# A second pair of buffers for the weights of a filler, and two more for the probabilities

## The chip, the cores and the metric

The kernel runs on one core of a Trainium2 chip, as one program. The metric is the time of one execution on the device in microseconds (us). Its engines are TensorE (PE, with its weight loads as PEld), VectorE (DVE), ScalarE (ACT) and GpSimd (POOL); SyncE (SP) issues the transfers. Each has its own queue of instructions and runs it in order, and semaphores make one wait for another.

## What is computed

One step of a small diffusion backbone with two layers, over 256 context tokens and 1024 latent tokens of width 1024. A layer normalizes, projects to three mixers (a long convolution by FFT, a short convolution, and latent attention with 8 heads), normalizes the mixers' outputs group by group, projects them with one matrix `w_out`, adds that to the residual, and then runs a gated feed-forward part. The part that matters here, from the reference:

```
s = jnp.einsum('bqhd,bkhd->bhqk', qi, kf) * scale
p = jax.nn.softmax(s, axis=-1)
return jnp.einsum('bhqk,bkhd->bqhd', p, vf)
...
y = jnp.concatenate([rmsnorm(y_hy, gg[:D_HYENA]),
                     rmsnorm(y_sc, gg[D_HYENA:D_HYENA + D_SCONV]),
                     rmsnorm(y_at, gg[D_HYENA + D_SCONV:])], axis=-1)
x = x + g1 * (y @ P['w_out'][l])
```

## The kernel before

The 1280 tokens stand in three chunks: latent tokens in chunks 0 and 1 (512 each), the context in chunk 2 (256). A product in fp32 is made of three matmuls: each operand is split in a high part (a cast on ACT) and a low part (a subtract on DVE), and `mm3` (L354) multiplies high by high, high by low and low by high.

Attention (`mla`, `attend`) goes head by head and block by block. For each tile of 128 keys PE makes the scores `st` in three matmuls, ACT takes the exponential into a `pt` buffer (L1292), POOL adds `pt` to a running sum (L1295), and PE multiplies pairs of `pt` by the values into `y` (L1277). At the end of a block `divide` makes the sums on PE (L1316), copies them (L1324, ACT), takes the reciprocal (L1325, DVE) and multiplies (L1326, POOL). Before the change `pt` has six buffers.

When a chunk's attention is complete, `group_norm` reads the mixers' outputs back from DRAM (`yd`), squares and adds them up (L500 and L503 on ACT, L504 on DVE), makes the reciprocal root per token with small matmuls (L526) and a run of tiny DVE steps (L376 to L383), spreads it over the partitions (L535 on DVE, L539 on PE), and scales, casts and splits the result (L1457, L1459, L1460).

The context chunk is complete first. Its projection by `w_out` is the filler: a generator that `mla` advances once in three key tiles while the last blocks of attention run; what is left of it when attention ends is drained. It has eight steps, one per 128 output columns. A step fetches its weight (512 KB, L336 on SP, into a ring of two raw slots), casts it into the high buffer `zo` (L344, ACT), subtracts into the low buffer (L345, DVE), runs 24 matmuls of 128x256 on PE (L354, output `pa`), and scales and adds the result on DVE (L1479), whose squares are summed for the next norm (L511 on ACT, L514 on POOL). Before the change there is one pair of `zo`, high and low, for all eight steps. Of the 24 matmuls the first two read the high buffer only.

Behind the filler stand the first weights of the latent projection (`zw`), then the group norm of a latent chunk, which needs the last division, and then that chunk's projection. The order on each engine is set by a scheduler from the order of the program, priorities and the buffers that are free. The names in rows: `arena` is the general store of temporary tiles, `operands` the split activations, `zo` and `zw` weight buffers, `pa` and `pb` accumulators.

Of the kernel before, what the change touches and what calls it, by code (L numbers as in the profile page):

```python
# [9 lines left out]
F32 = mybir.dt.float32  # L10
F32R = mybir.dt.float32r
# [41 lines left out]
FPOOL = ()  # L53
WPOOL = (1, 3, 5, 7)
# [181 lines left out]
class K:  # L236
# [45 lines left out]
    def open_z(self, part, use):  # L282

        g = self.tc.tile_pool(name="z" + part, bufs=1, reuse_waits="tile", side="left" if part == "a" else "right")
        pool = g.__enter__()
        self.zguard[part] = g

        def take(name, count, n, dt):
            return [Fixed(pool.tile([P, n], dt, name=f"{name}{i}"), n) for i in range(count)]

        if part == "a":
            if use == "start":
                self.zm, self.zd = take("zm", 2, 2048, F32), take("zd", 4, 1024, F32R)
            elif use == "attention":
                self.zkv = take("kv", 2, 4096, F32)
            elif use == "forms":
                self.zf = take("zf", 14, 512, F32R)
            else:
                self.zw = take("zw", 8, 1024, F32R)
        elif use == "attention":  # L300
            self.zp = take("pt", 6, 512, F32)
            self.zo = take("zo", 2, 1024, F32R)
        elif use == "forms":
            self.zg = take("zg", 9, 512, F32R)
            self.zq = take("zq", 5, 1024, F32R)
        else:
            self.zh = take("zh", 1, 2560, F32)
            self.ze = take("ze", 2, 2 * T, F32R)
# [1156 lines left out]
    def out_proj(self, l, cis, y, x, src, acc, early=(), dst=None):  # L1465

        nc = self.nc
        g1 = self.mod[l].v(2)[:, 16:24, :]
        for ci in cis:
            acc[ci] = None  # L1470
        for m in range(KD):
            w = self.load_split(early[m] if m < len(early) else self.i["w_out"][l, m], 1024, nc.gpsimd if m in (FPOOL if dst else WPOOL) else None, dst)
            for ci in cis:
                t0, n = CH[ci]
                xx = x[ci].f[:, n * m:n * m + n]
                nc.sync.dma_start(xx, src[:, m, t0:t0 + n])
                p = self.proj_tile(w, y, ci)
                s = 0 if ci < 2 else 1
                nc.vector.scalar_tensor_tensor(out=xx, in0=p[:, :n], scalar=g1[:, m, s:s + 1], in1=xx, op0=ALU.mult,  # L1479
                                               op1=ALU.add)  # L1480
                acc[ci] = self.add_square(acc[ci], xx, n, nc.vector if ONV else nc.gpsimd)
                if m % 2:
                    nc.sync.dma_start(self.xd[:, m - 1:m + 1, t0:t0 + n],
                                      x[ci].f[:, n * (m - 1):n * (m + 1)].rearrange("p (k n) -> p k n", n=n))
                self.tick()
            for b in w:
                b.free()
            yield
        for ci in cis:
            for b in (*y[ci][0], *y[ci][1]):  # L1490
                b.free()
# [557 lines left out]
```

## Time and profile before

| what | value |
|---|---|
| runs timed | 3701.41, 3706.76 (median), 3712.45 us |
| profiled execution | 3703.83 us, its span 3701.8 us |
| mean granted TensorE clock | 0.957 of 2.4 GHz |
| PE busy | 3435.0 us, 93% |
| DVE, POOL, ACT busy | 63%, 39%, 34% |
| the filler's stretch, layer 0 | about 839 to 912 us of the span |
| the filler's stretch, layer 1 | about 2622 to 2694 us |

The profile page has the busy time of each engine, the chain of work that ended last, and groups of like instructions with the idle time of their engine ahead of them and what ended it. The timelines list single instructions, or runs of like ones, of one stretch with their start; a wait stands in brackets with the instruction that ended it. Idle time of an engine that nothing waits for costs nothing, so the waits of PE are what to look at, and the clock that it was granted.

### The profile page before, as it was taken

To read this page: it belongs to the slowest core of one execution; us is meant where nothing else is said; L and a number is where in the kernel's file an instruction comes from. 1 tells how busy PE (TensorE), PEld (TensorE's weight loads), DVE (VectorE), ACT (ScalarE), POOL (GpSimd) and SP (SyncE) were. 2 spreads that over 40 slices of the span, in tenths; PEclk is the share of its full clock that TensorE was granted. 3 is DMA by queue.
4 is the path that set the end of the run, shared out by engine and by line. 5 is a ranking of instruction groups with operands and counts; after the bars stand their busy time and mean duration, and the time that the engine had idled before them with its cause. 6 is when DMAs were issued, how large, how long until landed. Compare 5 with 4: busy or idle time off the path is not lost.

```text
span 3701.8 us, 45689 instructions
## 1 busy us (share of the span) xinstructions
PE 3435.0 (93%) x17264; PEld 2705.9 (73%) x17264; DVE 2337.1 (63%) x3478; ACT 1245.1 (34%) x2245; POOL 1440.2 (39%) x1097
## 2 busy tenths in 40 slices
PE   7799889997879999999998988999897999999999
PEld 4488865655758888888886886655575888888888
DVE  4657577765476777546667757777658433435666
ACT  3522345544332222221114224555433322222110
POOL 3402346664443333332223223666645323223221
PEclk9899989999989999999999999999898999999999
DMA  7611100013423434342212210000451222214221
GB/s 275 241 60 61 42 10 11 19 39 128 145 65 113 134 123 125 114 154 85 96 58 74 65 47 14 4 11 19 134 165 55 83 69 69 71 61 154 97 77 69
DMA packets 118888, 317.87 MB, mean 86 GB/s; under 512 B 11371, under 2 KB 33387, under 8 KB 112652
## 3 DMA queue, kind: packets, MB, share of 16 engines
q1 hardware_dynamic: 118668, 314.96, 25.7%
q8 instruction: 135, 2.21, 0.3%
q14 instruction: 85, 0.70, 0.1%
HBM read 247.22 MB, written 67.70 MB: 85 GB/s over the span
## 4 chain that ended last, share of the span: by engine, by line
PE 76%; DVE 13%; issue 2%; ACT 2%; POOL 1%; DMA 1%; SPq 0%; DVEq 0%; POOLq 0%; ACTq 0%
PE pb L354 18%; PE pb L362 17%; PE pa L354 14%; PE pa L362 11%; PE st L354 6%; PE y L1277 4%; PE pa L1219 2%; DVE arena L852 1%; DVE arena L853 1%; PE pa L539 1%; PE pa L1238 1%; DVE arena L381 1%; PE pa L1231 1%; PE pa L1221 1%; DVE arena L383 1%
## 5 line engine op out<-in xcount | busy, mean ns | idle before, releaser
L354 PE MATMUL pb<-operands,zw 128*128 128x512 f32 (+1 forms) x2520 | 513.0, 361 | 5.7 <-DVE zw L345 3.0
L354 PEld LDWEIGHTS pb<-operands,zw 128*128 128x128 f32 x2520 | 427.1, 190 | 79.2 <-DVE zw L345 4.9
L362 PE MATMUL pb<-operands,zq 128*128 128x512 f32 (+1 forms) x2467 | 472.5, 348 | 5.5 <-DVE zq L1529 5.5
L1521 POOL TENSOR_TENSOR arena<-arena 128x512 f32<-128x512 f32 x176 | 262.1, 1491 | 523.3 <-DVE zq L1529 506.4
L1528 ACT CAST zq<-arena 128x512 fp32r<-128x512 f32 x356 | 220.8, 621 | 670.0 <-PE pb L362 428.4
L362 PEld LDWEIGHTS pb<-operands,zq 128*128 128x128 f32 x2467 | 391.7, 191 | 70.0 <-DVE zq L1529 6.9
L1529 DVE TENSOR_TENSOR zq<-arena,zq 128x512 fp32r<-128x512 f32 x356 | 288.7, 816 | 181.8 <-ACT zq L1528 177.6
L1295 POOL TENSOR_TENSOR arena<-pt,arena 128x512 f32<-128x512 f32 x256 | 334.7, 1307 | 93.7 <-ACT pt L1292 80.8
L354 PE MATMUL pa<-operands,zw 128*128 128x512 f32 (+1 forms) x1704 | 359.8, 368 | 1.1 <-DVE arena L558 0.6
L354 PEld LDWEIGHTS pa<-operands,zw 128*128 128x128 f32 x1704 | 296.2, 192 | 57.6 <-issue 3.6
L354 PE MATMUL st<-operands 97*128 97x512 f32 (+1 forms) x1056 | 321.0, 409 | 11.1 <-ACT pt L1292 11.1
L362 PE MATMUL pa<-operands,zq 128*128 128x256 f32 (+1 forms) x1801 | 320.8, 334 | 4.2 <-DVE zq L1529 4.2
L362 PEld LDWEIGHTS pa<-operands,zq 128*128 128x128 f32 x1801 | 272.5, 190 | 43.4 <-DVE zq L1529 4.9
L1708 DVE SCALAR_TENSOR_TENSOR arena<-pb,arena 128x512 f32<-128x512 f32 (+1 forms) x330 | 216.4, 661 | 115.4 <-PE pb L354 115.4
L1292 ACT ACTIVATE pt<-st 128x512 f32<-128x512 f32 (+1 forms) x352 | 202.4, 578 | 224.0 <-PE st L354 208.9
L354 PEld LDWEIGHTS st<-operands 97*128 97x128 f32 x1056 | 189.8, 196 | 116.0 <-issue 73.1
L344 ACT CAST zw<-arena 128x1024 fp32r<-128x1024 f32 x102 | 106.5, 1047 | 445.6 <-PE pb L354 374.4
L1277 PE MATMUL y<-pt,kv 128*64 128x512 f32 (+1 forms) x704 | 192.0, 616 | 0.0
L1220 DVE TENSOR_REDUCE arena<-pa 128x1 f32<-128x512 f32 x256 | 168.1, 686 | 34.8 <-PE pa L1219 30.7
L1708 DVE SCALAR_TENSOR_TENSOR arena<-pa,arena 128x512 f32<-128x512 f32 (+1 forms) x198 | 130.9, 661 | 92.8 <-PE pa L354 92.3
L362 PE MATMUL pb<-zf,zq 128*128 128x512 f32 x661 | 175.4, 403 | 10.5 <-DVE arena L1615 10.5
L354 PE MATMUL pb<-ze,zw 128*128 128x512 f32 (+1 forms) x900 | 182.4, 357 | 0.0
(279 smaller groups left out, 5576.6 us busy)
## 6 DMA issues: line engine op xcount, KB each, us to landing
hd<-arena SPq DMA_DIRECT2D x110, 256.0 KB, 2.1
zm<-in_w_modk SPq DMA_DIRECT2D x24, 1024.0 KB, 6.1
arena<-in_w_out SPq DMA_DIRECT2D x48, 512.0 KB, 3.6
arena<-in_w_mod SPq DMA_DIRECT2D x48, 512.0 KB, 3.5
arena<-in_w_g SPq DMA_DIRECT2D x44, 512.0 KB, 3.6
arena<-in_w_u SPq DMA_DIRECT2D x44, 512.0 KB, 3.6
arena<-in_w_dn SPq DMA_DIRECT2D x44, 512.0 KB, 3.8
arena<-hd SPq DMA_DIRECT2D x12, 1280.0 KB, 5.5
```

Of the source, the lines that this page charges most:

```text
L344: nc.scalar.copy(hi.r, raw.f)
L354: self.nc.tensor.matmul(out, a, b, start=(j == 0), stop=(j == n - 1))
L362: self.nc.tensor.matmul(out, a, b, start=(j == 0 and not add), stop=(j == n - 1), skip_group_check=add)
L1219: nc.tensor.matmul(p, q, kh[:96, 512 * c:512 * c + 512], start=True, stop=True)
L1220: v.reduce_max(out=mx[:, t, c:c + 1], in_=p, axis=AX.X)
L1277: ins = nc.tensor.matmul(y[64 * e:64 * e + 64, :n], G["kv"][:, kt0 + k + e, h, 0:64], pts[k + e].f[:, :n], start=(k == 0), stop=(k == nkt ...
L1292: ex = nc.scalar.activation(pt.f[:, :n], st[:, :n], AF.Exp)
L1295: (v if k in KDV else gp).tensor_tensor(out=acc.f[:, :n], in0=pt.f[:, :n], in1=(acc if k > 1 else pts[0]).f[:, :n], op=ALU.add)
L1521: gp.tensor_tensor(out=S[n].f, in0=a, in1=b, op=op)
L1528: nc.scalar.copy(f.r[:, 0:512], src)
L1529: v.tensor_tensor(out=f.r[:, 512:1024], in0=src, in1=f.f[:, 0:512], op=ALU.subtract)
L1708: nc.vector.scalar_tensor_tensor(out=xx, in0=p[:, :n], scalar=g2[:, m, q:q + 1], in1=xx, op0=ALU.mult, op1=ALU.add)
```

## The change

In the attention the ring of `pt` gets eight buffers instead of six, and `zo` four instead of two. The projection takes the first pair of `zo` for even steps and the second for odd ones. All of it fits in the memory that stands free during attention. The number of instructions on each engine stays as it is.

```
         elif use == "attention":
-            self.zp = take("pt", 6, 512, F32)
-            self.zo = take("zo", 2, 1024, F32R)
+            self.zp = take("pt", 8, 512, F32)
+            self.zo = take("zo", 4, 1024, F32R)
...
         for m in range(KD):
-            w = self.load_split(early[m] if m < len(early) else self.i["w_out"][l, m], 1024, nc.gpsimd if m in (FPOOL if dst else WPOOL) else None, dst)
+            w = self.load_split(early[m] if m < len(early) else self.i["w_out"][l, m], 1024, nc.gpsimd if m in (FPOOL if dst else WPOOL) else None, dst[2 * (m % 2):2 * (m % 2) + 2] if dst else None)
```

The instructions stand in another order only in the filler's stretch of each layer. On DVE in layer 0, from the first step's subtract to the fourth's, before (3325 and 3326 are the high and the low buffer):

```order
L345 TENSOR_TENSOR zo_3326<-arena,zo_3325 128x1024
L504 TENSOR_TENSOR arena<-arena 128x512
L1479 SCALAR_TENSOR_TENSOR arena<-pa,arena 128x256
L345 TENSOR_TENSOR zo_3326<-arena,zo_3325 128x1024
L1479 SCALAR_TENSOR_TENSOR arena<-pa,arena 128x256
L345 TENSOR_TENSOR zo_3326<-arena,zo_3325 128x1024
L504 TENSOR_TENSOR arena<-arena 128x512
L1325 RECIPROCAL arena<-arena 128x512
L1479 SCALAR_TENSOR_TENSOR arena<-pa,arena 128x256
L528 TENSOR_SCALAR arena<-pa 128x4
L345 TENSOR_TENSOR zo_3326<-arena,zo_3325 128x1024
```

And now, where 3327 and 3328 are the first pair and 3329 and 3330 the second:

```order
L345 TENSOR_TENSOR zo_3328<-arena,zo_3327 128x1024
L504 TENSOR_TENSOR arena<-arena 128x512
L345 TENSOR_TENSOR zo_3330<-arena,zo_3329 128x1024
L1479 SCALAR_TENSOR_TENSOR arena<-pa,arena 128x256
L345 TENSOR_TENSOR zo_3328<-arena,zo_3327 128x1024
L1479 SCALAR_TENSOR_TENSOR arena<-pa,arena 128x256
L345 TENSOR_TENSOR zo_3330<-arena,zo_3329 128x1024
L1325 RECIPROCAL arena<-arena 128x512
L1479 SCALAR_TENSOR_TENSOR arena<-pa,arena 128x256
```

The second subtract stands ahead of the first eviction (L1479), and the fourth ahead of the reciprocal.

On POOL at the same place, where the sums of the block before are divided (L1326), before:

```order
L514 TENSOR_TENSOR arena<-arena 128x256
L1295 TENSOR_TENSOR arena<-pt_3324,pt_3323 128x512
L1295 TENSOR_TENSOR arena<-pt_3319,arena 128x512
L1326 TENSOR_TENSOR arena<-arena 128x512
L1295 TENSOR_TENSOR arena<-pt_3320,arena 128x512
L514 TENSOR_TENSOR arena<-arena 128x256
L1295 TENSOR_TENSOR arena<-pt_3321,arena 128x512
L1521 TENSOR_TENSOR arena<-arena 128x512
```

And now:

```order
L514 TENSOR_TENSOR arena<-arena 128x256
L1326 TENSOR_TENSOR arena<-arena 128x512
L514 TENSOR_TENSOR arena<-arena 128x256
L1295 TENSOR_TENSOR arena<-pt_3326,pt_3325 128x512
L1295 TENSOR_TENSOR arena<-pt_3319,arena 128x512
L1521 TENSOR_TENSOR arena<-arena 128x512
```

Three adds of probabilities have moved from between the two L514 to behind them.

On PE in layer 0, the end of step 2 and the start of step 3, before, with scores and the values' pair just ahead:

```order
L354 MATMUL st<-operands 128x512 x5
L354 MATMUL pa<-operands,zo_3325 128x256 x2
L1316 MATMUL pa<-arena 64x512 x2
L526 MATMUL pa<-arena 128x1
L354 MATMUL pa<-operands,zo_3326 128x256
```

And now, with step 2 in the second pair and step 3 in the first:

```order
L354 MATMUL pa<-operands,zo_3329 128x256 x2
L354 MATMUL pa<-operands,zo_3330 128x256
L354 MATMUL pa<-operands,zo_3327 128x256 x2
L1316 MATMUL pa<-arena 64x512 x2
L354 MATMUL pa<-operands,zo_3328 128x256
```

Steps 2 and 3 follow each other directly, and the five matmuls for scores have gone from between them. Steps 4 and 5 do the same behind L539, and steps 7 and 8 at the end.

## Rows read from the trace of the kernel before

**Rows 1.** The page: busy us (share of the span) and number of instructions.

```profile
PE 3435.0 (93%) x17264; PEld 2705.9 (73%) x17264; DVE 2337.1 (63%) x3478; ACT 1245.1 (34%) x2245; POOL 1440.2 (39%) x1097
```

**Rows 2.** The filler's groups: busy us, mean ns | idle us before, what ended it.

```profile
L354 PE MATMUL pa<-operands,zo 128*128 128x256 f32 x384 | 59.3, 311 | 22.0 <-DVE zo L345 13.4 <-ACT zo L344 8.4 <-DVE arena L1457 0.2
...
L344 ACT CAST zo<-arena 128x1024 fp32r<-128x1024 f32 x16 | 16.7, 1046 | 25.9 <-PE pa L354 25.8
```

**Rows 3.** Timeline of PE, layer 0, steps 1 to 3: start us, us, instruction [idle before].

```profile
842.06 2.88 PE L354 MATMUL pa<-operands,zo 128*128 128x256 f32 x22 [0.45 <-DVE zo L345]
...
847.89 2.78 PE L354 MATMUL pa<-operands,zo 128*128 128x256 f32 x22
...
852.12 1.08 PE L1316 MATMUL pa<-arena 128*64 128x512 f32 x4
```

**Rows 4.** Timeline of PE, layer 0, from the norm of a latent chunk on.

```profile
868.77 1.05 PE L526 MATMUL pa<-arena 128*128 128x1 f32 x8 [2.91 <-DVE arena L504]
...
876.21 3.01 PE L539 MATMUL pa<-arena 128*128 128x512 f32 x6 [1.44 <-DVE arena L535]
...
888.95 5.07 PE L354 MATMUL pa<-operands,zo 128*128 128x256 f32 x22 [4.84 <-DVE zo L345]
894.93 0.51 PE L354 MATMUL pa<-operands,zo 128*128 128x256 f32 x2 [0.92 <-ACT zo L344]
896.19 2.88 PE L354 MATMUL pa<-operands,zo 128*128 128x256 f32 x22 [0.75 <-DVE zo L345]
...
905.66 1.08 PE L1316 MATMUL pa<-arena 128*64 128x512 f32 x4
...
933.35 5.46 PE L539 MATMUL pa<-arena 128*128 128x512 f32 x6 [3.40 <-DVE arena L535]
```

**Rows 5.** Timeline of all engines, layer 1, the same stretch.

```profile
2636.09 1.08 PE L1316 MATMUL pa<-arena 128*64 128x512 f32 x4
...
2657.14 3.96 PE L539 MATMUL pa<-arena 128*128 128x512 f32 x6
...
2669.40 2.28 DVE L345 TENSOR_TENSOR zo<-arena,zo 128x1024 fp32r<-128x1024 f32 x1
...
2671.73 4.33 PE L354 MATMUL pa<-operands,zo 128*128 128x256 f32 x22 [3.93 <-DVE zo L345]
...
2678.24 4.06 PE L354 MATMUL pa<-operands,zo 128*128 128x256 f32 x22 [0.76 <-DVE zo L345]
...
2688.78 1.08 PE L1316 MATMUL pa<-arena 128*64 128x512 f32 x4
```

**Rows 6.** Timeline of DVE, layer 0, step 5's subtract.

```profile
887.15 1.74 DVE L345 TENSOR_TENSOR zo<-arena,zo 128x1024 fp32r<-128x1024 f32 x1
```

**Rows 7.** Windows: PE, PEld, DVE, ACT, POOL busy us, PEclk, DMA share, GB/s.

```profile
884.00:888.00 4.00, 0.10 (x1) 0.00 (x0) 4.00 (x6) 2.43 (x5) 2.90 (x3) 0.94 0.98 333
888.00:892.00 4.00, 3.05 (x14) 3.05 (x15) 1.49 (x2) 0.00 (x0) 0.00 (x0) 0.50 0.74 223
...
896.00:900.00 4.00, 2.88 (x22) 2.68 (x22) 1.31 (x3) 2.22 (x4) 0.73 (x1) 1.00 0.43 131
```

**Rows 8.** The group of the exponentials, columns as in rows 2.

```profile
L1292 ACT ACTIVATE pt<-st 128x512 f32<-128x512 f32 (+1 forms) x352 | 202.4, 578 | 224.0 <-PE st L354 208.9 <-POOL arena L1295 8.0
```

**Rows 9.** The page's transfers of w_out: KB each, median us to landing.

```profile
arena<-in_w_out SPq DMA_DIRECT2D x48, 512.0 KB, 3.6
```

**Rows 10.** Timeline of all engines, layer 0, between reciprocal and squares.

```profile
859.37 2.28 POOL L1326 TENSOR_TENSOR arena<-arena 128x512 f32<-128x512 f32 x1
...
861.61 1.27 POOL L1295 TENSOR_TENSOR arena<-pt,arena 128x512 f32<-128x512 f32 x1
...
862.84 0.74 POOL L514 TENSOR_TENSOR arena<-arena 128x256 f32<-128x256 f32 x1
...
863.61 0.63 ACT L500 ACTIVATE arena<-arena 128x512 f32<-128x512 f32 x1 [2.15 <-POOL arena L514]
```

**Rows 11.** The tile zo, its subtracts: ns min/median/max, first and last start.

```profile
L345 DVE TENSOR_TENSOR zo<-arena,zo x16: 1224/1226/2279, 840.4 to 2688.3; 128x1024 fp32r<-128x1024 f32 x16
```

## The prediction

> **What bounds the kernel now.** The page comes first: TensorE (PE) is busy 93% of the span and the chain that ended last lies on it [rows 1], so time can only be won where PE stands idle, or runs at the lower clock, beside something that the change touches. Next the groups of the filler's instructions: its 384 matmuls have 22.0 us of idle time ahead of them, nearly all put down to the weight's subtract on DVE (13.4) and its cast on ACT (8.4), and the cast in turn waits 25.8 us for PE, that is for the only pair of zo buffers [rows 2]. This is a loop: matmuls of step m, cast of m+1, subtract of m+1, matmuls of m+1. Then the timelines of the two stretches, one per layer, show where the 22 us lie. In the first steps PE has attention scores (st) and values (y) to run meanwhile, and hardly waits [rows 3]. From the context chunk's end on that work is used up: in layer 0 step 5 waits 4.84 us, and steps 6 to 8 wait some 0.9 us before their first two matmuls and 0.75 before the other 22 [rows 4]; layer 1 has 3.93 us and the same short waits [rows 5]. The long wait has DVE's order behind it: the subtract could not be written before PE had left step 4's buffers, and by then DVE had the norm's work ahead of it, so it ran at 887.15 [rows 6]. The windows show what follows such a wait: PE 0.10 us busy in 884 to 888, then a granted clock of 0.50, which is 1.2 of 2.4 GHz, in 888 to 892 [rows 7]; those 22 matmuls took 5.07 us instead of 2.88.
>
> **What the change moves.** Nothing is added: the instructions are the same in number and size. Two things move. (1) With a second zo pair the cast of step m+1 waits for the matmuls of m-1. In the order, DVE now subtracts step 2's weight ahead of step 1's eviction, and PE runs steps 1, 2 and 3 in a row, the scores and values that stood between them behind, 30 st matmuls and 6 y pairs, unchanged in sum. (2) Eight pt buffers let the exponentials run two tiles further ahead. In the attention proper PE's order does not change, and all waits of exp for POOL are 8.0 us over 352 instructions, beside 208.9 for PE [rows 8]: none of it is shown to reach PE. I cost that at 0 to 2 us of gain and take 0, the nearer row being that exp mostly waits for PE.
>
> **Layer 0, step by step.** Step 1's matmuls are gated as before and end at 842.06 + 2.88 = 844.94 [rows 3]. Step 2's 24 follow in 2.78 + 0.25 (two more matmuls at 0.126), and two of step 3 take 0.25: the L1316 pair, which stands behind them, starts at about 848.3 instead of 852.12, 3.8 earlier. Is the weight there? Step 2's cast no longer waits for PE and its subtract (1.2 to 1.7 us) stands behind one L504 of 0.7, done near 844. Step 3's transfer starts when step 1's subtract frees the raw slot, about 842, lands 3.6 us later [rows 9], and its cast (1.05) waits for step 1 to end, so it is done near 846.7, before the two matmuls that need it; its subtract is done near 848, before the other 22. The cover is thin, about 1 us.
>
> From L1316 to the third L526 the trace has 852.12 to 868.77. In this chain L1326 on POOL stood behind an add and took 2.28 us, then came another add (1.27) and the L514 that L500 waited for until 863.61 [rows 10]. In the new order POOL has L514, L1326, L514 in a row, without adds. So: copy and reciprocal end at about 853.7 (6.4 us behind L1316 before, some 5.4 now that less stands ahead on ACT and DVE), L1326 1.3 to 2.3, L514 0.74: L500 near 856.1, 7.5 earlier. From L500 to the third L526 it was 5.16, from there to L539 7.44 [rows 4]; both parts are DVE's and stay. L539 starts at about 868.7. PE meanwhile runs 19 st, 3 pairs and two L526 until about 861, then waits some 3.4 us ahead of L539, 2 more than the 1.44 now.
>
> From L539 to the next L1316 it was 905.66 - 876.21 = 29.45. Out of this go the waits, 1.06 + 4.84 + 0.92 + 0.75 + 1.02 + 0.76 + 1.02 = 10.37 (those of steps 5 to 8; of the repeated short ones two rows stand in [rows 4]), and 5.07 - 2.88 = 2.19 of low clock. Into it come step 8's 22 matmuls, which stood behind L1316 (2.9), and 6 st and 2 pairs, 1.6 + 2.2. Steps 4 and 5 are now both loaded before the norm's DVE work, run in a row, and cover it with 6.2 us of PE time; step 6's subtract, behind step 5's eviction (0.48), needs 1.7 us, and the three st and a pair standing there give 1.9. Sum: 29.45 - 10.37 - 2.19 + 6.7 = 23.6. With up to 2.2 for low clock behind the wait ahead of L539 I take 24.9: L1316 at 893.6, 12 earlier. Behind it stands the same chain of sums, reciprocal, last norm and L539, some 32 us on which nothing is taken away, with its own low clock (L539 5.46 us at 933.35 [rows 4]). Gain of layer 0: 12, between 9 and 16.
>
> **Layer 1.** The same steps: by the same links the first L1316 comes 3.7 before 2636.09; the next link is longer by a little, since POOL had no add there before and now has two ahead of the second L514, so the third L526 gains only about 2.5; ahead of L539 PE itself was late (no idle before 2657.14), so that gains 4 [rows 5]. From L539 to the next L1316 it was 31.64; the waits (3.93 and five short ones, 8.3 together) and the low clock of two steps (1.47 and 1.20) go [rows 5], 2.9 for step 8 and 3.5 for later st and y come in: 27.0, so L1316 is 8.6 earlier. Behind it POOL has the first subtract of the next weights (2.4 us) ahead of L1326, which may cost up to 2 of this. Gain 8.5, between 5 and 12.
>
> **Weighing the subtracts.** They last 1226 ns at the median and 1.74 or 2.28 where POOL works at the same time [rows 5, 6, 11]. This is what the Trainium skill says in SBUF — State Buffer, section "SBUF: two separate sides": VectorE and GpSimd share a port pair under an exclusive lock, and an operation of either fully blocks the other. The rule speaks against a change that pulls subtracts in among POOL's adds, and the trace agrees (2.28 against 1.23). If all six that move forward cost the 1.05 more on the path, the sum would lose 6.3; by the rows they lie beside 3 us of matmuls each, and it loses none.
>
> **The sum.** 12 + 8.5 = 20.5 us, made against the profiled execution: 3703.83 - 20.5 = 3683.3. That run lies 2.93 under the median of the three (3706.76), so the same change on the median gives 3686. Bounds: 9 + 5 = 14 and 16 + 12 + 2 = 30, that is 3677 to 3693.
>
> **Rivals.** What a measurement of this kernel can tell from no change is about 0.3%, 11.1 us, so "faster" means under 3695.6.
>
> *Only the short waits go.* The steps close up, but the norm's chain does not come earlier, and the long waits move to it: what is lost at step 5 is waited ahead of L539. Then the short waits are the gain, 4.5 in layer 0 and 4.4 in layer 1: 8.9 us, 3698. For it: PE waits for DVE at L526 and L539 today as well [rows 4]. Against it: L1316 stands behind the filler's matmuls, which come earlier in any case, and POOL's order loses two adds from the chain.
>
> *The raw ring decides.* It still has two slots: a transfer of weight m+2 starts only when subtract m has ended. Landing 3.6 [rows 9], cast 1.05 and subtract 1.23 make 5.9 us per two steps, 2.9 a step against 3.0 for 24 matmuls: it just holds. If transfers land in 5 us beside others, a step costs 3.7, 0.6 more over some 14 steps, and two long waits come back: 0 to 8 us of gain, 3699 to 3707. By the Trainium skill, TensorE: Matmul & The Clock Gate, section "HAM oscillation — how this bites in real kernels", double-buffering one more level brought no further gain in a kernel that had been rearranged to keep PE fed; for this kernel that would be this case. The trace speaks against it by the 25.8 us for which casts waited for PE and not for a transfer [rows 2].
>
> *Slower: the clock.* Three steps in a row take the scores and values away from where they covered the norm, PE waits longer ahead of L539, and what follows runs at 1.2 GHz. That decides if the granted clock stays near 0.5 from L539 to step 8 in both layers: five steps then cost 4.4 - 2.9 + 0.2 more each, L539 2.45 more, 11 a layer, 22 in all, against 8.9 of short waits won: 3720. Against it: in layer 0 the clock is back at 1.00 by 896 although short waits go on [rows 7].
>
> **Chances.** Forecast 0.70 (gain 11 to 28); only the short waits 0.15 (a third of it past 11 us, as chains partly come earlier); raw ring, or the buffers free nothing, 0.08; slower by the clock 0.04; more than forecast, over 28, 0.03. Faster 0.70 + 0.05 + 0.03 = 0.78, same 0.10 + 0.08 = 0.18, slower 0.04. The range that leaves out about 2 in 10 goes from 3675 (gain 31) to 3700 (gain 7).
>
> **What would show it.** In the changed profile: casts of zo wait for PE under 8 us instead of 25.8; the zo matmuls' idle falls from 22.0 to under 6; no wait over 2 us at step 5 in either layer; first L1316 of layer 0 about 3.8, L500 7.5, L539 7.5 and second L1316 12 us earlier; the exponentials' waits and the attention before 838 unchanged. Wrong would be: an idle over 5 us ahead of L539, step 3 waiting for its weight, or a second L1316 that is less than 5 us earlier.

## The result and the profile after

The changed kernel takes 3681.86 us (median of 4 runs, 3675.49 to 3687.47) beside 3709.26 for the kernel before on the same chip (4 runs). The ratio is 0.994, with a 95% interval from 0.9922 to 0.9957: between 16 and 29 us less, 22 by the ratio and 27 by the medians. Forecast were 3686 us and 20.5 us less, in a range from 3675 to 3700.

The groups of the filler in the whole trace after, columns as in [rows 2]:

```profile
L354 PE MATMUL pa<-operands,zo 128*128 128x256 f32 x384 | 48.7, 284 | 2.8 <-DVE zo L345 1.7 <-ACT zo L344 1.1
...
L344 ACT CAST zo<-arena 128x1024 fp32r<-128x1024 f32 x16 | 16.8, 1047 | 11.0 <-DMA arena<-in_w_out 8.8 <-PE pa L354 2.2
```

Of 22.0 us of idle time 2.8 are left, and the casts wait for PE no longer (2.2 against 25.8 us), but for transfers (8.8). The matmuls themselves are shorter too, 48.7 against 59.3 us in sum: they no longer follow long waits at the lower clock. Now the timeline of PE in layer 0, to be read beside [rows 3] and [rows 4]:

```profile
849.85 5.96 PE L354 MATMUL pa<-operands,zo 128*128 128x256 f32 x48 [0.45 <-DVE zo L345]
855.74 1.08 PE L1316 MATMUL pa<-arena 128*64 128x512 f32 x4
...
869.53 1.00 PE L526 MATMUL pa<-arena 128*128 128x1 f32 x8
...
879.58 4.91 PE L539 MATMUL pa<-arena 128*128 128x512 f32 x6 [5.12 <-DVE arena L535]
...
885.03 6.09 PE L354 MATMUL pa<-operands,zo 128*128 128x256 f32 x50
...
895.13 8.24 PE L354 MATMUL pa<-operands,zo 128*128 128x256 f32 x68
903.31 1.08 PE L1316 MATMUL pa<-arena 128*64 128x512 f32 x4
...
929.28 5.46 PE L539 MATMUL pa<-arena 128*128 128x512 f32 x6 [3.40 <-DVE arena L535]
```

The filler runs in blocks of 48, 50 and 68 matmuls without a wait inside, and the long wait of step 5 is gone. In its place stands a wait of 5.12 us ahead of the first L539 (1.44 before). In layer 1:

```profile
2619.12 5.96 PE L354 MATMUL pa<-operands,zo 128*128 128x256 f32 x48 [1.13 <-DVE zo L345]
2625.01 1.08 PE L1316 MATMUL pa<-arena 128*64 128x512 f32 x4
...
2648.45 4.51 PE L539 MATMUL pa<-arena 128*128 128x512 f32 x6 [1.78 <-DVE arena L535]
...
2672.98 1.03 PE L1316 MATMUL pa<-arena 128*64 128x512 f32 x4
...
2691.68 2.93 PE L539 MATMUL pa<-arena 128*128 128x512 f32 x6
```

The two traces can't be laid over each other by their starts. The first zo matmul of layer 0 starts at 848.19 after and at 840.41 before, 7.8 us later, although nothing ahead of it was moved on PE: 3.3 us come in the first 130 us, and 3.1 between 615 and 680, where PE waits as long in both (5.61 and 5.57 us), but the granted clock in 12 us around those waits is 0.52 after and 0.72 before. The low clock falls on other instructions from run to run; that this makes the scatter of some 12 us among runs of one kernel is likely, but two traces do not show it. So each link is measured from the first zo matmul of its layer (2623.02 before and 2617.49 after in layer 1):

| link, us from the first zo matmul | layer 0 before | after | moved | forecast | layer 1 before | after | moved | forecast |
|---|---|---|---|---|---|---|---|---|
| first L1316 | 11.7 | 7.6 | -4.2 | -3.8 | 13.1 | 7.5 | -5.6 | -3.7 |
| third L526 | 28.4 | 21.3 | -7.0 | -7.5 | 27.2 | 22.6 | -4.6 | -2.5 |
| L539 of the first norm | 35.8 | 31.4 | -4.4 | -7.5 | 34.1 | 31.0 | -3.2 | -4 |
| second L1316 | 65.3 | 55.1 | -10.1 | -12 | 65.8 | 55.5 | -10.3 | -8.6 |
| last L539 | 92.9 | 81.1 | -11.9 | -12 | 86.2 | 74.2 | -12.0 | -8.5 |

Both stretches gain 12 us, 23.9 together. The span of the profiled run is 16.4 less, since 7.8 were lost ahead of the first stretch, and between and behind the two it differs by another -1.5 and +1.2.

### The profile page after: what moved, and what is told of

It is laid out like the page before. It is cut to its first block, busy times and chain, and to the rows that moved or that the text cites. A ratio compares the mean times of both kernels' runs of the same rounds, so it can differ in the third digit from the quotient of the medians.

```text
span 3685.4 us, 45693 instructions
## 1 busy us (share of the span) xinstructions
PE 3434.4 (93%) x17264; PEld 2703.4 (73%) x17264; DVE 2338.0 (63%) x3478; ACT 1243.3 (34%) x2245; POOL 1441.5 (39%) x1097
## 4 chain that ended last, share of the span: by engine, by line
PE 75%; DVE 12%; issue 2%; ACT 2%; DMA 2%; POOL 2%; SPq 0%; DVEq 0%; ACTq 0%; POOLq 0%
PE pb L354 18%; PE pb L362 17%; PE pa L354 14%; PE pa L362 11%; PE st L354 6%; PE y L1277 4%; PE pa L1219 2%; DVE arena L852 1%; PE pa L539 1%; DVE arena L853 1%; PE pa L1238 1%; DVE arena L381 1%; PE pa L1231 1%; PE pa L1221 1%; DVE arena L382 1%
```

## The experiments

All times below are medians beside the kernel before on the same chip (3701 to 3705 us in these sets); the ratio is to that kernel, with its 95% interval.

**e1, the second pair alone.**

```
-            self.zp = take("pt", 8, 512, F32)
+            self.zp = take("pt", 6, 512, F32)
```

> Two pairs of zo as in the change, but six pt buffers as before. Theory: the second zo pair alone makes the gain. The order on PE in both filler stretches is that of the changed kernel, so the time is that of the changed kernel within noise, 22 us under before (ratio 0.994, 0.992 to 0.996), and the zo matmuls' idle is near 2.8 us, as there. Rival: the two further pt buffers carry a part, by letting the exponentials run ahead; then this one is at least 4 us slower than the changed kernel, 18 us or less under before.

3680.11 us beside 3705.03, ratio 0.9929 (0.9914 to 0.9943); the zo matmuls' idle is 3.3 us. The order on PE in both stretches is that of the changed kernel. The second pair makes the gain.

**e2, eight probability buffers alone.**

```
-            self.zo = take("zo", 4, 1024, F32R)
+            self.zo = take("zo", 2, 1024, F32R)
...
-            w = self.load_split(..., dst[2 * (m % 2):2 * (m % 2) + 2] if dst else None)
+            w = self.load_split(..., dst)
```

> Eight pt buffers, one pair of zo as before. Theory: no gain, 3707 us and a ratio within 0.999 to 1.001; the zo matmuls keep 22 us of idle, the casts keep 26 us of waiting for PE; the exponentials' waits for POOL fall from 8.0 to about 5.6 us as in the changed kernel, without effect on PE. Rival: the exponentials' lead reaches PE; then 4 us or more faster than before.

3703.84 us beside 3705.03, ratio 0.9996 (0.9987 to 1.0006). The filler's group waits as before:

```profile
L354 PE MATMUL pa<-operands,zo 128*128 128x256 f32 x384 | 60.7, 316 | 21.3 <-DVE zo L345 13.6 <-ACT zo L344 7.6 <-DVE arena L1457 0.2
```

The two further buffers are worth nothing that can be measured.

**e3, two high buffers and one low.**

```
-            self.zo = take("zo", 4, 1024, F32R)
+            self.zo = take("zo", 3, 1024, F32R)
...
-            w = self.load_split(..., dst[2 * (m % 2):2 * (m % 2) + 2] if dst else None)
+            w = self.load_split(..., (dst[m % 2], dst[2]) if dst else None)
```

> Two high buffers, one low: the cast of the next weight can run ahead, its subtract has to wait for the matmuls of the step before. Theory (the subtract's place in DVE's order is what costs): the short waits for casts go (8.4 of the 22.0 us), those for subtracts stay (13 us, with waits of 4 to 5 us at step 5 behind the norm's work on DVE), so about a third to a half of the gain: 8 to 13 us under before, 3694 to 3699. Rival: the loop is broken as soon as the cast runs ahead, since the subtract is only 1.2 us; then as fast as the changed kernel, 20 us or more under before.

3696.41 us beside 3705.03, ratio 0.9976 (0.9963 to 0.999): 9 us, a third to two fifths of the gain. Its group, and PE behind the norm in layer 0:

```profile
L354 PE MATMUL pa<-operands,zo 128*128 128x256 f32 x384 | 51.9, 291 | 15.1 <-DVE zo L345 13.3 <-ACT zo L344 1.7
```

```profile
893.42 4.26 PE L354 MATMUL pa<-operands,zo 128*128 128x256 f32 x22 [4.05 <-DVE zo L345]
899.38 3.11 PE L354 MATMUL pa<-operands,zo 128*128 128x256 f32 x24 [1.71 <-DVE zo L345]
```

The waits for casts are gone (8.4 to 1.7 us), those for subtracts are as before (13.3), the one of 4 us at step 5 among them. What the change pays for is mostly the subtract: with a buffer of its own it stands ahead of the norm's work on DVE.

**e4, the group norms' small steps through PSUM.** The expected link that came short is L526 to L539. In the trace after, the small steps of the reciprocal root on DVE in layer 0 begin so, beside POOL's adds of probabilities:

```profile
870.76 1.05 DVE L376 TENSOR_SCALAR arena<-arena 128x12 int32<-128x12 int32 x1
871.85 1.21 DVE L377 TENSOR_SCALAR arena<-arena 128x12 int32<-128x12 int32 x1
873.09 0.17 DVE L381 SCALAR_TENSOR_TENSOR arena<-arena 128x12 f32<-128x12 f32 x1
873.29 1.14 DVE L382 TENSOR_TENSOR arena<-arena 128x12 f32<-128x12 f32 x1
874.47 0.17 DVE L383 SCALAR_TENSOR_TENSOR arena<-arena 128x12 f32<-128x12 f32 x1
```

```profile
871.75 6.73 POOL L1295 TENSOR_TENSOR arena<-pt,arena 128x512 f32<-128x512 f32 x5
```

Six of the eleven steps last 1.05 to 1.21 us instead of 0.17, about one for each of POOL's instructions. They also end with them: POOL's instructions end at 871.79, 873.03, 874.40 and 875.76, and the first four long steps 0.02 to 0.03 us later. Before, only three steps were long (1.12 to 1.28 us), for POOL's adds ended at 874.09. So the stretch from the end of L526 to the first L535 takes 8.2 us instead of 5.5. The edit keeps the number of the instructions, and lets each of these steps, and the spread behind them (the old L535), read at most one operand from SBUF and one from PSUM. The scheduler moved a few instructions with it: on PE in layer 0 three matmuls for scores stand ahead of the first zo matmuls instead of behind them, and in layer 1 more have moved.

```
-        self.rsqrt_of(y, rs.f[:, 0:nt * na], nt * na)
+        if na > 1:
+            u, s = st[:, 128:128 + n0], rs.f[:, 0:n0]
+            v.tensor_scalar(out=u.bitcast(I32), in0=xs.bitcast(I32), scalar1=1, ..., op0=ALU.logical_shift_right)
...
+                v.scalar_tensor_tensor(out=u, in0=xs, scalar=-0.5, in1=s, op0=ALU.mult, op1=ALU.mult)
+                v.tensor_tensor(out=u, in0=u, in1=s, op=ALU.mult)
...
+                v.scalar_tensor_tensor(out=(y if it == 2 else s), in0=u, scalar=1.5, in1=s, ...)
```

Here `st` (with `xs` and `u` in it) is the accumulator tile in PSUM, and `s` stands in SBUF. The first two steps (L376 and L377) read a single operand already before the edit, from SBUF; now they read it from PSUM.

> The changed kernel with the group norms' small reciprocal-root steps (128x12) working through PSUM, so that each reads one operand at most from SBUF; the same number of instructions in the same order. In the changed kernel these steps and the gap between them take 8.2 us in layer 0 and 5.3 in layer 1 (before: 5.5 and 3.4), with single steps of 1.1 instead of 0.17 us wherever POOL is adding probabilities. Theory: these long steps wait for POOL's hold on the memory port that both share. Then no step is over 0.5 us, the run takes 2 to 3 us, L539 of layer 0 comes about 5 us earlier against the first zo matmul and that of layer 1 about 2, and the time is 3 to 8 us under the changed kernel: 25 to 30 under before, ratio 0.992. Rival: the long steps come from their waits on each other or from instruction issue; then they stay near 1.1 us and the time is that of the changed kernel.

3673.34 us beside 3705.03, ratio 0.9906 (0.989 to 0.9921). The same place in its trace, all engines (its L535 to L542 are the small steps, L548 the old L535, L1308 the adds, L552 the old L539):

```profile
861.09 0.18 DVE L535 TENSOR_SCALAR pa<-pa 128x12 int32<-128x12 int32 x1
861.30 0.17 DVE L536 TENSOR_SCALAR arena<-pa 128x12 int32<-128x12 int32 x1
861.41 6.70 POOL L1308 TENSOR_TENSOR arena<-pt,arena 128x512 f32<-128x512 f32 x5
861.51 0.18 DVE L538 SCALAR_TENSOR_TENSOR pa<-pa,arena 128x12 f32<-128x12 f32 x1
861.72 0.18 DVE L539 TENSOR_TENSOR pa<-pa,arena 128x12 f32<-128x12 f32 x1
...
863.40 1.28 DVE L548 TENSOR_TENSOR arena<-arena,pa 128x512 f32<-128x512 f32 x2
...
865.29 2.93 PE L552 MATMUL pa<-arena 128*128 128x512 f32 x6
```

With POOL's adds running beside them no step is over 0.18 us, the run takes 2.5 us, and from the third L526 (859.90) to L539 it is 5.4 us, against 10.05 in the changed kernel and 7.44 before. L539 comes 28.1 us behind the first zo matmul (837.16 here): 7.7 earlier than before. That this is near the 7.5 that was forecast is chance, since the 48 matmuls ahead of L1316 ran partly at the lower clock in this run (8.29 us instead of 5.96). The long steps were waits on memory that POOL holds, as the theory had it: the rival, waits on each other or on issue, would have left them near 1.1 us. The Trainium skill has the rule in SBUF — State Buffer, section "SBUF: two separate sides": the port pair that VectorE and GpSimd share is locked for a whole instruction. The trace agrees, and adds that it strikes steps of 12 elements as hard as long ones (0.9 to 1.0 us each, against 1.05 for a subtract of 128x1024 [rows 5]).

**e5, the filler once in four key tiles.**

```
-FILL = 3
+FILL = 4
```

> The changed kernel with the filler advanced once in four key tiles instead of three, so that two to three of its eight steps come behind attention's last sums (L1316). Theory: from the last L1316 to the last L539 a chain of DVE, ACT and a transfer runs some 26 to 30 us, in which PE idles 13.6 us in layer 0 of the changed kernel; L1316 comes 66 matmuls (8 us) earlier against the L539 before it, 44 of them cover idle time behind it, and 24 are left behind the last L539. Gain 2 to 5 us per layer, 3 to 9 under the changed kernel. Rival: the steps behind L1316 put their subtracts and evictions into DVE's chain and take back what was won; then within 2 us of the changed kernel.

3685.87 us beside 3704.5, ratio 0.9953 (0.9937 to 0.9968): not better than the changed kernel, by the medians 4 us worse. The theory fell in layer 1. In layer 0 the profiled run is 4.6 us shorter from the first zo matmul to the context's next L539 (116.1 against 120.7 us), as forecast; in layer 1 the same stretch is 13.7 longer (121.6 against 107.9), where PE stands so behind the last L1316:

```profile
2656.62 1.03 PE L1316 MATMUL pa<-arena 128*64 128x512 f32 x4
2657.58 1.05 PE L526 MATMUL pa<-arena 128*128 128x1 f32 x8
2663.44 2.17 PE L354 MATMUL pb<-operands,zw 128*128 128x512 f32 x4 [4.81 <-ACT zw L344]
2666.82 1.65 PE L354 MATMUL pb<-operands,zw 128*128 128x512 f32 x3 [1.21 <-POOL zw L345]
```

The latent projection's first matmul stands 6.8 us behind L1316, where it stood 3.4 behind it in the changed kernel, and waits for its weight; what follows runs at the lower clock for a while (17 matmuls in 6.72 us at 2673.67, where 24 took 5.75 in layer 0 of the changed kernel).

**e6, the filler once in two key tiles.** The same line with FILL = 2.

> The changed kernel with the filler advanced once in two key tiles. Now five steps run in a row before the first L1316, 70 matmuls (8.7 us) more than in the changed kernel, and two steps fewer are left to cover the norm's work behind L539. Theory (what counts is where the two divisions stand, not how many waits of the filler are gone): the first L1316 and the L539 behind it come 6 to 9 us later against the first zo matmul, the second L1316 about as in the changed kernel, since 46 fewer matmuls stand between; total within 4 us of the changed kernel, not better by more than 2. Rival: steps in a row are what pays, so more of them pay more; then 4 us or more under the changed kernel.

3677.13 us beside 3704.5, ratio 0.9928 (0.991 to 0.9946): as the changed kernel. In layer 0 the first L1316 stands 18.8 us behind the first zo matmul (7.6 in the changed kernel) and L539 41.8 (31.4), more than forecast, but the second L1316 54.5 (55.1). In layer 1 the second L1316 does not stay: 61.3 against 55.5, the last L539 76.5 against 74.2, and yet the run is no slower. More steps in a row pay nothing; that the second division sets the end fits layer 0 alone.

**e7, three raw slots.**

```
-                    self.open_rings(raw=("f", 1024, 2))
+                    self.open_rings(raw=("f", 1024, 3))
```

> The changed kernel with three raw slots instead of two for the filler's weights as they land. In the changed kernel the casts of zo wait 8.8 us for transfers, but the zo matmuls on PE only 2.8 us. Theory: the raw ring is not what bounds it; the casts' wait for transfers falls under 3 us and the time stays within 3 us of the changed kernel. Rival (the raw ring decides, in part): 5 us or more under the changed kernel.

3679.84 us beside 3704.5, ratio 0.9929 (0.991 to 0.9949). The casts wait for no transfer any more, and the time stays:

```profile
L344 ACT CAST zo<-arena 128x1024 fp32r<-128x1024 f32 x16 | 16.7, 1045 | 8.1 <-PE pa L354 5.3 <-issue 2.7
```

A third slot gains nothing that can be measured. The scheduler set another order with it (the first L1316 of layer 0 stands 12.8 us behind the first zo matmul instead of 7.6), so the run does not show that the transfers cost nothing in the order of the changed kernel; one of them does cost there, as told below.

**e8, e4 and e5 together** (PSUM steps and FILL = 4).

> Both: the norms' small steps through PSUM, and the filler advanced once in four key tiles. The two act on different links (L526 to L539 of the first norm; the stretch behind the last L1316), so by the theories their gains add: 9 us of the first and 3 to 9 of the second, 3663 to 3670 beside 3705 of the kernel before. Rival: with the norm's chain shorter, DVE's order behind it is the next bound and the second adds nothing; then 3671 to 3675.

3678.93 us beside 3704.5, ratio 0.9936 (0.9919 to 0.9952): a miss for the theory, and worse than its rival. It is 6 us worse than e4 alone by the medians and 11 by the ratios, which is about the loss of e5.

**e9, the PSUM steps of e4 with one zo pair** and six pt buffers, as before.

> The kernel before (one zo pair, six pt) with the group norms' small steps through PSUM. There four of these steps lay under POOL's adds (three of 1.1 to 1.3 us in layer 0, one of 1.2 in layer 1), against nine in the changed kernel (six and three). Theory: the change moved the norm's small steps under POOL's adds and so gave back part of its gain; then the same remedy is worth 4 us here and 9 there, 3698 to 3703 beside 3705 before. Rival: the remedy is worth the same in both, 7 us or more here; then the change gave nothing back, and the two are simply added.

3710.03 us beside 3704.58, ratio 1.001 (1.0 to 1.002). Both theories miss: the remedy is worth nothing here. PE in layer 0, L552 being the old L539:

```profile
874.76 3.03 PE L552 MATMUL pa<-arena 128*128 128x512 f32 x6
...
887.52 4.55 PE L354 MATMUL pa<-operands,zo 128*128 128x256 f32 x22 [4.85 <-DVE zo L345]
```

The small steps are short (2.5 us), but PE has scores and values to run until 874.76. Ahead of this L539 only 1.44 us of waiting stood before, and none in layer 1, so no more than that could be won; and step 5 waits 4.85 us for its subtract, as before. Steps 5 to 7 ran at the lower clock in this run (4.55, 4.39 and 4.39 us, where only step 5 did before), which can hide a gain of that size. So what is won on DVE is hardly on the path while the filler waits for its own buffers.

**e10, the PSUM steps in every norm that has them** (the condition `na > 1` left out of e4).

> The changed kernel with PSUM for the small steps in every norm that has them, not the group norms alone. The other norms stand where POOL adds no probabilities. Theory: as with the group norms alone, within 3 us, 3671 to 3676 beside 3705 before. Rival: the small steps wait for POOL's other work in those norms too; then 4 us or more faster than with the group norms alone.

3642.99 us beside 3704.58, ratio 0.9824 (0.9806 to 0.9842): the theory fell, the rival holds, and by far. It is the fastest version here, 62 us under before. The norms elsewhere meet other work of POOL, here in the changed kernel in layer 1, DVE:

```profile
2767.59 0.16 DVE L528 TENSOR_SCALAR arena<-pa 128x4 f32<-128x4 f32 x1
2767.79 2.31 DVE L376 TENSOR_SCALAR arena<-arena 128x4 int32<-128x4 int32 x1
2770.14 1.19 DVE L377 TENSOR_SCALAR arena<-arena 128x4 int32<-128x4 int32 x1
2771.36 1.18 DVE L381 SCALAR_TENSOR_TENSOR arena<-arena 128x4 f32<-128x4 f32 x1
```

A subtract of POOL lasts from 2767.73 to 2770.07, and a shift of four numbers beside it 2.31 us. The wait ahead of this norm's L539 was 9.30 us and is 3.28 in e10. Over the whole trace, the changed kernel first, then e10:

```profile
L539 PE MATMUL pa<-arena 128*128 128x512 f32 (+1 forms) x60 | 40.2, 800 | 58.1 <-DVE arena L535 55.4 <-issue 2.2 <-PE pa L539 0.4
```

```profile
L552 PE MATMUL pa<-arena 128*128 128x512 f32 (+1 forms) x60 | 31.8, 647 | 21.6 <-DVE arena L548 21.6
```

36.5 us of PE's idle time go, and the matmuls themselves take 8.4 us less. Of the idle time 7.7 us had gone with e4 (50.4 left there).

**e11, e4 with three raw slots and FILL = 4.**

> The changed kernel with the group norms' small steps through PSUM, three raw slots and the filler once in four key tiles. With one in four, layer 0 was 4 to 5 us faster, but in layer 1 the first zw weights came late (waits of 4.8, 1.2 and 3.3 us on PE), since the filler's last weights held the two raw slots. Theory: a third slot lets them land earlier; then layer 1 loses less and the time is near that of the PSUM kernel alone or under it, 3666 to 3674 beside 3705. Rival: the late weights come from the casts' and subtracts' place in the order, not from the slots; then as with once in four and PSUM, 3677 to 3681.

3682.04 us beside 3704.58, ratio 0.9938 (0.9924 to 0.9951): the rival holds. The third slot does not mend e5. One cast of zw in layer 1 still waits 1.27 us for its transfer; the longer waits of PE name casts and subtracts (in layer 0 5.0 us for the subtract of zw), so the late weights come mostly from their order.

**e12, the PSUM steps in every norm with one zo pair** and six pt buffers.

> PSUM for the small steps of every norm, with one zo pair and six pt buffers as before. It tells how the 62 us of the version with both edits divide. Theory: the norms outside attention gain their 30 us whatever zo does, the group norms gain nothing with one pair (as measured), and the second pair is worth what it was and the 8 us of the group norms more: 3672 to 3678 beside 3705 before, 29 to 35 us slower than with both. Rival: the norms' gain needs the second pair as well; then 3690 or more.

3679.74 us beside 3701.53, ratio 0.9939 (0.9926 to 0.9953): 22 us where 27 to 33 were forecast: a miss of the theory, though far from the rival. The gain of the other norms is not the same whatever zo does: it was 30 us from e4 to e10. The zo matmuls wait 27.6 us in this run. With both edits it is 62 us, so they help each other: the second pair is worth 22 to 27 us without the PSUM steps and, from 0.9939 to 0.9824, some 40 with them. The intervals leave this only just clear of a plain sum, and no run shows which wait it comes from.

## Why the prediction was right, and where not

The mechanism is the one forecast: one pair of buffers tied cast, subtract and matmuls into a loop, and the second pair opens it (e1 against e2; waits 22.0 to 2.8 us). That pt is worth nothing was said and holds (e2). The sum of both layers was forecast at 20.5 us; the stretches gained 23.9, the runs 22 by the ratio.

Point by point. First L1316 of layer 0: forecast 3.8 earlier, measured 4.2. In layer 1 5.6 instead of 3.7, because step 1's 22 matmuls ran at the lower clock before and not after; that is a chance of the run, not the change, for in e3 the 24 of this step took 3.13 us behind the same wait (1.12 us):

```profile
2624.65 4.41 PE L354 MATMUL pa<-operands,zo 128*128 128x256 f32 x22 [1.11 <-DVE zo L345]
```

L500 [rows 10] and the third L526 of layer 0: 7.5 forecast, 5.8 (863.61 before, 865.57 after) and 7.0 measured. L500 fell short because the L514 ahead of it waited and took longer than the 0.74 us of the forecast:

```profile
862.64 1.05 ACT L344 CAST zo<-arena 128x1024 fp32r<-128x1024 f32 x1 [2.93 <-DMA arena<-in_w_out]
863.60 0.41 ACT L511 ACTIVATE arena<-arena 128x256 f32<-128x256 f32 x1
864.15 1.39 POOL L514 TENSOR_TENSOR arena<-arena 128x256 f32<-128x256 f32 x1 [1.09 <-ACT arena L511]
865.57 0.63 ACT L500 ACTIVATE arena<-arena 128x512 f32<-128x512 f32 x1 [1.08 <-POOL arena L514]
```

A cast of zo waits 2.93 us for its weight's transfer, the square L511 stands behind it on ACT, and L514 waits 1.09 us for that square; it then runs beside a subtract of DVE (863.73 to 864.96) and takes 0.65 us more. The forecast of this link had no transfer in it. The small subtract waits of steps 6 to 8 are gone, as is the long wait in both layers.

The step that failed is the one "from L500 to the third L526 it was 5.16, from there to L539 7.44; both parts are DVE's and stay". Neither did. The first took 3.96 us: POOL's adds had mostly gone from beside its three L504 sums (0.69, 0.69 and 1.17 us, where the three took 4.44 before). The second took 10.05 us, and L539 came 4.4 earlier instead of 7.5, with 5.12 us of waiting ahead of it instead of 3.4 (the text named an idle over 5 us there as a sign of error). The adds now ran beside the norm's small steps. The forecast had weighed that contention for the subtracts of 128x1024 only, where it did not matter, and not for eleven steps in a row, each of which can wait for one add. e4 shows it: without that contention the second part takes 5.4 us, and no wait is left ahead of L539.

The links behind it made up for most: from L539 to the second L1316 it was 23.7 us, forecast 24.9 with up to 2.2 of low clock, and from there to the last L539 26.0 against 27.7 before, where nothing had been forecast. There POOL's first subtract of the next weights stood between the last reciprocal and its L1326 before; now it is done (907.53) before the reciprocal ends. Before, then after:

```profile
911.18 2.41 POOL L345 TENSOR_TENSOR zw<-arena,zw 128x1024 fp32r<-128x1024 f32 x1 [4.15 <-ACT zw L344]
913.54 1.29 POOL L1326 TENSOR_TENSOR arena<-arena 128x512 f32<-128x512 f32 x1
```

```profile
905.11 2.42 POOL L345 TENSOR_TENSOR zw<-arena,zw 128x1024 fp32r<-128x1024 f32 x1 [1.70 <-ACT zw L344]
909.43 1.28 POOL L1326 TENSOR_TENSOR arena<-arena 128x512 f32<-128x512 f32 x1 [1.21 <-DVE arena L1325]
```

L1326 starts 6.1 us behind L1316 instead of 7.9. In layer 1 the whole gave 12.0 instead of 8.5: some 1.5 is the clock of step 1, and 1.7 the last link, on which no gain had been forecast there either. That layer 0 came out at 11.9 us against 12 is thus partly luck: a loss and a gain, neither of them forecast, cancel.

The rivals. "Only the short waits go" (8.9 us) falls with the second L1316, 10 us earlier in both layers; e3 comes near it in size, with 9, but there the long wait of step 5 stays. "The raw ring decides" falls with the gain and with e7; one transfer shows in L500 all the same. "Slower: the clock" did not come. The windows around the wait ahead of L539, columns as in [rows 7], show the low clock, and its end before step 4 starts at 885:

```profile
876.00:880.00 4.00, 0.42 (x1) 0.45 (x2) 3.84 (x6) 0.00 (x0) 2.40 (x2) 0.62 0.00 0
880.00:884.00 4.00, 4.00 (x7) 1.45 (x6) 2.37 (x5) 0.91 (x2) 0.26 (x1) 0.52 0.00 0
884.00:888.00 4.00, 4.00 (x31) 3.62 (x30) 3.29 (x6) 2.51 (x6) 3.00 (x3) 1.00 0.13 19
```

After such waits L539 takes 4.91 us instead of 3.01, and that is all it costs. Of the first of them one part came true, a longer wait ahead of L539, but by e4 it is POOL's adds that made it so long.

## What to carry to other kernels

Where two engines prepare an operand for a third in one buffer, look for the group whose idle time names them in turn, and ask behind what the preparing instruction would queue if it could not start early; most of the gain came with the second low buffer (e3), where the subtract otherwise stood behind a norm. A chain of tiny VectorE steps is priced by what GpSimd does beside it, not by its own size: read the longest of them, not the median, and give each step one operand in PSUM. An edit off the path is worth nothing until the wait that hides it is gone (e9 against e4), so measure such edits together too.

## What the runs showed of the hardware that was not expected

A step of DVE on 4 or 12 numbers per partition lasts 0.16 to 0.18 us by itself and up to 2.31 us while POOL runs a 128x1024 subtract (2.34 us), and 1.05 to 1.28 us in a row of POOL's 1.3 us adds; with one operand in PSUM it is 0.16 to 0.18 beside the same work (e4, e10). Steps with a single SBUF operand (L376, L377) wait as well as those with two. And the low clock falls on different waits from run to run: with an unchanged order and waits of 5.57 and 5.61 us, one stretch of layer 0 differed by 3.1 us between two runs (granted clock 0.72 and 0.52 in 12 us).
